# A decoder trunk on one core: parameters loaded late, first weights loaded early, eight unused matmuls

## The chip, the cores and the metric

The kernel runs on one core of one Trainium2 chip. TensorE does matmuls and transposes, VectorE, ScalarE and GpSimd do the element-wise work, and SyncE (SP) issues nearly all loads; each engine works through its own instructions in order. The metric is the device time of one execution in microseconds (us), as the median of several runs.

## The reference

One layer of a hybrid decoder in float32, 1024 tokens of width 1024:

```python
h = rms_norm(x, norm_mix_g[l], NORM_EPS)
z = h @ w_in[l]                          # 1024 x 2048: pool inputs, q, k, v
y_pool = pooling_mixer(zp, pool_w[l], pool_scale[l])
lam = exp(sum(lambda_q1 * lambda_k1)) - exp(sum(lambda_q2 * lambda_k2)) + lam_init
o = diff_attention(q, k, v, lam, rel_bias)   # 4 heads, two softmax maps each
o = rms_norm(o, subln_g[l], SUBLN_EPS) * (1.0 - lam_init)
x = x + concatenate([y_pool, o]) @ w_out[l]
h = rms_norm(x, norm_ffn_g[l], NORM_EPS)
gu = h @ ffn_w_in[l]                     # 1024 x 5632
g = causal_depthwise_conv(gu[..., :D_FF], ffn_conv_w[l], ffn_conv_b[l])
x = x + (silu(g) * gu[..., D_FF:]) @ ffn_w_out[l]
return rms_norm(x, norm_final_g, NORM_EPS)
```

## The kernel before, in words

Each float32 product is made of three matmuls: operands are split into a high part (a cast, on ScalarE) and a low part (a subtraction, on GpSimd for weights, on VectorE for what comes out of a PSUM bank), and `mm3` (L143 to L145) adds high x high, high x low and low x high.

The kernel goes through these stages: the row tiles of x are normalised and transposed, and the q, k and v projections of head 0 run as tiles become ready; then attention of four heads, interleaved with the other projections and the pooling; the output projection in three groups; the second normalisation; the gated MLP, upward and downward. The names and lines that the change touches are all in the first stage.

Row tiles. x0 to x7 are 128 tokens each (tile `x`, four buffers, so x4 needs x0's buffer, and x6 that of x2). For each tile ScalarE squares and sums it (L116, `sq`), VectorE and ScalarE make the reciprocal root (L118 to L122, L108 to L111), VectorE scales the tile (L130; for x5 and x7 L127, with GpSimd multiplying by the norm's weights at L128). TensorE transposes it in two groups of four (L139) into PSUM tiles `tp` (two buffers), ScalarE copies each out as `hTh` (L83) and VectorE makes `hTl` (L84). A buffer of `tp` is free again when its low part is made.

First projections. `q0`, `k0` and `v0` (tiles `raw`, `whi`, `wlo`) are the weights of head 0. `first_units` runs their projections `z_q`, `z_k`, `z_v`: for the first four tiles in pairs of tiles (256 columns), for the last four at once (512 columns). They are copied out at L285, L286 (q), L299 to L301 (k) and L314, L317 (v, with one more transpose `tpv`).

Small parameters. `load_params` loads the relative bias `rel_bias` (`rb`), a one-hot table (`oh`), a row with the lambdas and the far bias broadcast to all partitions (`flat`), and rows with convolution and norm weights (`prow`). `small_params` makes of them a bias row `r_ps` (L194, written to DRAM and read back per head as `hank`), the transposed parameters `prm` (L199, L200), `recfar` (L202) and the factor `nlam` (L206 to L211). The first attention step needs the bias and `nlam`.

Order. `LOADS` is the order in which the first loads are issued. The order of the rest is that in which the code records it, rearranged by a scheduler; `tc.high_priority()` moves a piece forward. `ws` holds `raw` once and `whi`, `wlo` twice, so the weights of head 1 wait for the last use of q0's.

Of the kernel before, what the change touches and what calls it, by code (L numbers as in the profile page):

```python
# [19 lines left out]
NT = S // P  # L20
# [11 lines left out]
QK = 10  # L32
OUT_GROUPS = ((3, 2), (1, 0, 4), (5, 6, 7))
FIRST = ("q0", "k0", "v0")
LOADS = "x0 g x1 x2 q0 k0 s x3 v0"
SHARE = (5, 7)
PLAN = ("b0 a00 a01 q1 a02 k1 v1 a03 b1 p3 a10 q2 a11 a12 v2 a13 k2 p2 b2 a20 a21 q3 p0 a22 p1 a23 v3 k3 "
        "b3 a30 a31 a32 a33")
# [4 lines left out]
def trunk_kernel(ctx, tc, x, norm_mix_g, w_in, pool_w, rows, line, rel_bias, w_out, norm_ffn_g,  # L43
                 ffn_w_in, ffn_w_out, norm_final_g, onehot, out):
    nc = tc.nc
# [16 lines left out]
    def slot(dt, name):  # L62
        return slots.tile([P, S], dt, tag="y", name=name)

    def sc_ps(name):
        return ps_a.tile([P, 512], F32, tag="sc", bufs=3, name=name)

    def pv_ps(name):
        return ps_a.tile([P, 512], F32, tag="pv", bufs=1, name=name)

    def tp_ps(name):
        return ps_a.tile([P, 4, P], F32, tag="tp", bufs=2, name=name)
# [5 lines left out]
    def split(hi, lo, src, lo_eng=None):  # L78
        nc.scalar.copy(hi, src)  # L79
        (lo_eng or nc.gpsimd).tensor_tensor(lo, src, hi.bitcast(F32), op=ALU.subtract)  # L80

    def psplit(hi, lo, src):
        nc.scalar.copy(hi, src)  # L83
        nc.vector.tensor_tensor(lo, src, hi.bitcast(F32), op=ALU.subtract)  # L84
# [9 lines left out]
    def split_w(raw, name):  # L94
        if name == "v0":
            hi, lo = [slot(F32R, f"{n}_{name}").rearrange("p (k c) -> p k c", c=P) for n in ("whi", "wlo")]
        else:
            hi = ws.tile([P, KC, P], F32R, tag="whi", name=f"whi_{name}")
            lo = ws.tile([P, KC, P], F32R, tag="wlo", name=f"wlo_{name}")
        split(hi, lo, raw)  # L100
        return hi, lo
# [23 lines left out]
    def scale_rows(dst, src, r, g, share):  # L125
        if share:
            nc.vector.tensor_scalar(dst, src, r, None, op0=ALU.mult)  # L127
            nc.gpsimd.tensor_tensor(dst, dst, g, op=ALU.mult)  # L128
        else:
            nc.vector.scalar_tensor_tensor(dst, src, r, g, op0=ALU.mult, op1=ALU.mult)  # L130

    def to_channels(xn, hi, lo, t, name):
        for q in range(2):
            if name == "f" and q:
                tp = sc_ps(f"tp_{name}_{t}_{q}").rearrange("p (k c) -> p k c", c=P)
            else:
                tp = tp_ps(f"tp_{name}_{t}_{q}")
            for k in range(4):
                nc.tensor.transpose(tp[:, k, :], xn[:, (4 * q + k) * P:(4 * q + k + 1) * P], ident)  # L139
            psplit(hi[q][:, :, t * P:(t + 1) * P], lo[q][:, :, t * P:(t + 1) * P], tp)  # L140
# [26 lines left out]
    def load_x(t):  # L167
        xt = att.tile([P, D], F32, tag="p", bufs=4, name=f"x_{t}")
        nc.sync.dma_start(xt, x[t * P:(t + 1) * P, :])
        return xt  # L170


    prow = att.tile([96, P], F32, tag="ln", bufs=2, name="prow")
    flat = att.tile([P, 276], F32, tag="hank", bufs=1, name="flat")
# [4 lines left out]
    oh = att.tile([33, 512], F32, tag="ln", bufs=2, name="oh")  # L179

    def load_params():
        nc.vector.memset(rb[32:33, :], NEG)
        nc.sync.dma_start(rb[0:32, :], rel_bias)
        nc.sync.dma_start(oh, onehot)
        nc.sync.dma_start(flat, line.to_broadcast((P, 276)))
        nc.sync.dma_start(prow[0:93, :], rows)
# [5 lines left out]
    def small_params():  # L192
        r_ps = sc_ps("r_ps")
        nc.tensor.matmul(r_ps[0:NH, :], rb, oh, start=True, stop=True)  # L194
        r_sb = att.tile([NH, 512], F32, tag="vt", bufs=1, name="r_sb")
        nc.vector.tensor_copy(r_sb, r_ps[0:NH, :])
        nc.sync.dma_start(scratch, r_sb)
        prm_ps = sc_ps("prm_ps")
        nc.tensor.transpose(prm_ps[:, 0:93], prow[0:93, :], ident[0:93, 0:93])  # L199
        nc.vector.tensor_copy(prm[:, 0:93], prm_ps[:, 0:93])  # L200
        nc.vector.tensor_scalar(gsub, prm[:, 92:93], 1.0 - LAM_INIT, None, op0=ALU.mult)
        nc.vector.tensor_copy(recfar, flat[:, 256:276])  # L202
        lam_s = const.tile([P, 2], F32, name="lam_s")
        lam_p = att.tile([P, 64], F32, tag="tb", bufs=1, name="lam_p")
        for j in range(2):
            nc.vector.tensor_tensor_reduce(lam_p, lam_in[:, 2 * j, :], lam_in[:, 2 * j + 1, :], 1.0, 0.0,  # L206
                                           ALU.mult, ALU.add, lam_s[:, j:j + 1])
        lam_e = const.tile([P, 2], F32, name="lam_e")
        nc.scalar.activation(lam_e, lam_s, AF.Exp)
        nc.vector.tensor_tensor(nlam, lam_e[:, 1:2], lam_e[:, 0:1], op=ALU.subtract)  # L210
        nc.vector.tensor_scalar(nlam, nlam, -LAM_INIT, None, op0=ALU.add)  # L211
# [6 lines left out]
    def load_step(s):  # L218
        if s[0] == "x":
            xs[int(s[1])] = load_x(int(s[1]))  # L220
        elif s == "g":
            nc.sync.dma_start(g_bc, norm_mix_g.to_broadcast((P, D)))
        elif s == "s":
            load_params()
        else:
            first_raw[s] = load_raw(w_in_src(dict(q0=4, k0=8, v0=12)[s]), s)

    xs, first_raw, first_w, first_evac, first_ps = {}, {}, {}, {}, {}
    for s in LOADS.split():
        load_step(s)  # L230
# [45 lines left out]
    def q_sink(h):  # L276
        q = [att.tile([P, S], F32R, tag="qk", bufs=QK, name=f"q{h}_{c}") for c in range(2)]

        def evac(half, ps):
            cs = slice(half * 512, half * 512 + 512)  # L280
            for c in range(2):
                hi = q[c][64 * c:64 * c + 64, cs]
                lo = q[c][64 - 64 * c:128 - 64 * c, cs]
                src = ps[64 * c:64 * c + 64, :]
                nc.scalar.mul(hi, src, SC)  # L285
                nc.vector.scalar_tensor_tensor(lo, src, SC, hi.bitcast(F32), op0=ALU.mult, op1=ALU.subtract)  # L286
        return q, evac

    def k_sink(h):
        kh = [(slot(F32R, f"kh{h}_{c}") if h == 1 else  # L290
               att.tile([P, S], F32R, tag="qk", bufs=QK, name=f"kh{h}_{c}")) for c in range(2)]
        kl = slot(F32R, f"kl{h}") if h == 1 else att.tile([P, S], F32R, tag="qk", bufs=QK, name=f"kl{h}")

        def evac(half, ps):
            cs = slice(half * 512, half * 512 + 512)
            for c in range(2):
                src = ps[64 * c:64 * c + 64, :]
                own = kh[c][64 * c:64 * c + 64, cs]
                nc.scalar.copy(own, src)  # L299
                nc.scalar.copy(kh[c][64 - 64 * c:128 - 64 * c, cs], src)  # L300
                nc.vector.tensor_tensor(kl[64 * c:64 * c + 64, cs], src, own.bitcast(F32), op=ALU.subtract)  # L301
        return (kh, kl), evac

    def v_sink(h):
        vh = att.tile([P, S], F32R, tag="qk", bufs=QK, name=f"vh{h}")
        if h == 1:
            vl = slot(F32R, f"vl{h}")
        else:
            vl = att.tile([P, S], F32R, tag="pl" if h == 3 else "qk", bufs=3 if h == 3 else QK, name=f"vl{h}")
        vh, vl = [a.rearrange("p (t e) -> p t e", e=P) for a in (vh, vl)]  # L310

        def evac(half, ps):
            vt = att.tile([P, 512], F32, tag="vt", bufs=1, name=f"vt{h}_{half}")
            nc.scalar.copy(vt, ps)  # L314
            tp = mm_ps(f"tpv{h}_{half}").rearrange("p (t e) -> p t e", e=P)
            for j in range(4):
                nc.tensor.transpose(tp[:, j, :], vt[:, j * P:(j + 1) * P], ident)  # L317
            psplit(vh[:, 4 * half:4 * half + 4, :], vl[:, 4 * half:4 * half + 4, :], tp)
        return (vh, vl), evac

    for t in range(NT):
        if t == 1:
            first_w.update({n: split_w(first_raw[n], n) for n in FIRST})
            q0, first_evac["q0"] = q_sink(0)
            k0, first_evac["k0"] = k_sink(0)
            v0, first_evac["v0"] = v_sink(0)
            small_params()
        if t not in xs:
            xs[t] = load_x(t)
        xt = xs[t]  # L330
        sq = att.tile([P, S], F32, tag="pl", bufs=3, name=f"sq_{t}")
        r = row_rstd(xt, sq, f"m{t}")
        scale_rows(xt, xt, r, g_bc, t in SHARE)
        with tc.high_priority():
            to_channels(xt, hTh, hTl, t, "m")
        if t % 2 == 1:
            first_units(t // 2)

# [163 lines left out]
    x1 = [None] * NT  # L502
# [317 lines left out]
```

## Time and profile before

| | |
|---|---|
| median of 3 runs | 1118.35 us (1118.02 to 1118.36) |
| the profiled execution: time | 1118.18 us |
| its span, first to last instruction | 1116.4 us |
| TensorE busy | 1068.5 us (96%) |
| VectorE busy | 725.4 us (65%) |
| ScalarE busy | 475.9 us (43%) |
| GpSimd busy | 337.4 us (30%) |
| mean granted TensorE clock | 0.984 |

Times in the rows are counted from the start of the span, so the profiled execution has 1.78 us around it. In the profile PE is TensorE, PEld its weight loads, DVE is VectorE, ACT is ScalarE, POOL is GpSimd, and SPq is SyncE's queue, on which loads are issued. A matmul's time in a row is from its start to the modelled end; since matmuls overlap, their pace is read from one start to the next. A granted clock below 1 is a stretch in which the clock was held at its lower level for a part of the time; the first 25 us show 1.00 in that column although the matmuls' pace there is that of the lower level, so the pace is what is read there.

### The profile page before, as it was taken

What the parts mean: (1) busy time and instruction counts of PE and PEld (TensorE: products, weight loads), DVE (VectorE), ACT (ScalarE), POOL (GpSimd) and SP (SyncE); (2) the same over time, 40 slices, a digit from 0 to 9 for tenths busy, and PEclk for the clock granted to TensorE, in tenths of its full rate; (3) what the DMA queues carried; (4) which work ended last, traced back from release to release, by engine and by line L of the source; (5) the groups of instructions that cost most, each with busy time, mean ns of one, the idle gap of its engine ahead of it and who ended that gap; (6) DMA issues with size and microseconds to landing.
All of it is one profiled execution on the core that took longest, in us unless ns stands there. A gap on an engine that the chain in (4) does not pass through costs nothing.

```text
span 1116.4 us, 13587 instructions
## 1 busy us (share of the span) xinstructions
PE 1068.5 (96%) x5011; PEld 885.4 (79%) x5011; DVE 725.4 (65%) x1213; ACT 475.9 (43%) x775; POOL 337.4 (30%) x240
## 2 busy tenths in 40 slices
PE   5999999999899897899999999999999999999997
PEld 4988888887778585778888888888888788888885
DVE  6556786878796589476657656755765655544545
ACT  5557476655762355244434443433444222111123
POOL 3232242432740237133322222221314322221211
PEclk9999999999899898899999999999999999999999
DMA  7111110100586642123122222222247632212112
GB/s 233 36 44 33 43 46 19 43 20 8 208 281 218 199 170 76 57 86 98 62 95 95 79 73 94 77 86 85 76 132 254 236 113 98 86 63 95 38 49 103
DMA packets 85990, 111.76 MB, mean 100 GB/s; under 512 B 3618, under 2 KB 66303, under 8 KB 85924
## 3 DMA queue, kind: packets, MB, share of 16 engines
q1 hardware_dynamic: 79300, 86.78, 24.2%
q10 hardware_dynamic: 6624, 24.12, 5.6%
q8 instruction: 39, 0.64, 0.2%
q14 instruction: 27, 0.22, 0.1%
HBM read 82.57 MB, written 28.32 MB: 99 GB/s over the span
## 4 chain that ended last, share of the span: by engine, by line
PE 82%; DVE 8%; ACT 3%; issue 3%; DMA 2%; POOL 1%; SPq 1%; DVEq 0%; ACTq 0%; POOLq 0%
PE p L644 36%; PE fo L741 7%; PE fo L742 7%; PE fo L743 7%; PE o L533 2%; PE o L532 2%; PE o L531 2%; PE z_q L144 1%; PE z_q L145 1%; PE z_q L143 1%; PE s L353 1%; PE s L352 1%; PE tpa L402 1%; PE z_p L143 1%; PE z_p L144 1%
## 5 line engine op out<-in xcount | busy, mean ns | idle before, releaser
L741 PE MATMUL fo<-w,a 128*128 128x512 f32 x352 | 137.3, 390 | 2.7 <-DVE xr L744 2.7
L744 DVE TENSOR_TENSOR xr<-xr,fo 128x512 f32<-128x512 f32 x112 | 75.9, 684 | 97.0 <-PE fo L743 96.3
L742 PE MATMUL fo<-w,a 128*128 128x512 f32 x352 | 137.0, 389 | 0.0
L743 PE MATMUL fo<-w,a 128*128 128x512 f32 x352 | 137.0, 389 | 0.0
L80 POOL TENSOR_TENSOR w<-rw,w 128x1024 fp32r<-128x1024 f32 x22 | 61.3, 2794 | 156.3 <-ACT w L79 156.3
L622 POOL TENSOR_TENSOR sa<-rg 128x512 f32<-128x512 f32 x22 | 33.4, 1519 | 209.6 <-DMA rg<-in_ffn_w_in_dram 209.6
L741 PEld LDWEIGHTS fo<-w,a 128*128 128x128 f32 x352 | 66.1, 188 | 17.5 <-DVE xr L744 3.9
L80 POOL TENSOR_TENSOR ul<-ru,uh 128x1024 fp32r<-128x1024 f32 x22 | 57.9, 2632 | 69.9 <-PE p L644 35.9
L743 PEld LDWEIGHTS fo<-w,a 128*128 128x128 f32 x352 | 66.1, 188 | 13.9
L742 PEld LDWEIGHTS fo<-w,a 128*128 128x128 f32 x352 | 66.1, 188 | 13.7
L79 ACT CAST a<-ra 128x1024 fp32r<-128x1024 f32 x22 | 23.2, 1052 | 119.8 <-PE fo L743 62.8
L362 ACT ACTIVATE p<-p,nm 128x128 f32<-128x128 f32 (+7 forms) x64 | 49.6, 776 | 50.4 <-DVE nm L361 47.7
L644 PE MATMUL p<-t4h,gt 128*128 128x512 f32 x176 | 58.0, 391 | 1.7 <-DVE g L669 1.7
L531 PE MATMUL o<-woh,yh 128*128 128x512 f32 x128 | 52.7, 417 | 5.0 <-ACT yh L79 4.2
L623 DVE TENSOR_TENSOR sa<-sa,ru 128x512 f32<-128x512 f32 x22 | 39.9, 1813 | 22.7 <-POOL sa L622 22.7
L349 POOL CAST qz<-q 64x128 fp32r<-64x128 f32 x64 | 23.6, 371 | 97.1 <-PE s L353 90.2
L533 PE MATMUL o<-woh,yl 128*128 128x512 f32 x128 | 51.9, 407 | 0.6 <-DVE yl L80 0.6
L532 PE MATMUL o<-wol,yh 128*128 128x512 f32 x128 | 52.2, 409 | 0.3 <-POOL wol L80 0.3
L79 ACT CAST uh<-ru 128x1024 fp32r<-128x1024 f32 x22 | 23.2, 1054 | 68.2 <-PE p L644 66.9
L80 DVE TENSOR_TENSOR a<-ra,a 128x1024 fp32r<-128x1024 f32 x22 | 42.9, 1948 | 12.2 <-ACT a L79 11.8
L671 DVE TENSOR_TENSOR g<-eb,p 128x512 f32<-128x512 f32 x22 | 15.1, 687 | 54.9 <-PE p L644 54.9
L534 DVE TENSOR_TENSOR x<-x,o 128x512 f32<-128x512 f32 x48 | 32.7, 684 | 20.4 <-PE o L533 18.5
(264 smaller groups left out, 3082.7 us busy)
## 6 DMA issues: line engine op xcount, KB each, us to landing
x_rows<-x ACTq DMA_DIRECT2D x24, 512.0 KB, 3.3
ru<-in_ffn_w_in_dram SPq DMA_DIRECT2D x22, 512.0 KB, 4.1
rg<-in_ffn_w_in_dram SPq DMA_DIRECT2D x22, 512.0 KB, 3.9
act_rows<-cv ACTq DMA_DIRECT2D x22, 512.0 KB, 3.0
rw<-in_ffn_w_out_dram SPq DMA_DIRECT2D x22, 512.0 KB, 4.2
ra<-act_rows SPq DMA_DIRECT2D x22, 512.0 KB, 3.4
x<-in_x_dram SPq DMA_DIRECT2D x16, 512.0 KB, 5.8
x<-x_rows SPq DMA_DIRECT2D x16, 512.0 KB, 3.9
```

The costliest lines, as they stand in the source:

```text
L79: nc.scalar.copy(hi, src)
L80: (lo_eng or nc.gpsimd).tensor_tensor(lo, src, hi.bitcast(F32), op=ALU.subtract)
L362: nc.scalar.activation(s[:, 0:w], s[:, 0:w], AF.Exp, bias=negm[:, c:c + 1], accum_out=sums[:, c:c + 1])
L531: nc.tensor.matmul(ps, yh[:, ts], wh[:, cs], start=n == 0, stop=False)
L532: nc.tensor.matmul(ps, yh[:, ts], wl[:, cs], start=False, stop=False)
L533: nc.tensor.matmul(ps, yl[:, ts], wh[:, cs], start=False, stop=n == len(wo) - 1)
L623: nc.vector.tensor_tensor(s2, s1, a11, op=ALU.subtract)
L644: nc.tensor.matmul(ps, w[:, k, :], h[:, k, :], start=start and k == 0 and n == 0, stop=k == 3 and n == 2, skip_group_check=not start)
L741: nc.tensor.matmul(ps, ah[:, ts], wh[:, cs], start=n == 0, stop=False)
L742: nc.tensor.matmul(ps, ah[:, ts], wl[:, cs], start=False, stop=False)
L743: nc.tensor.matmul(ps, al[:, ts], wh[:, cs], start=False, stop=n == len(ops) - 1)
L744: nc.vector.tensor_tensor(xr[t][:, cs], xr[t][:, cs], ps, op=ALU.add)
```

## The change

The first weights are loaded between the row tiles instead of after them, and the step `s` (`load_params`) leaves the list of first loads. Eight matmuls of q0's weights with themselves, whose result nothing reads, stand behind the splits of the first weights. `load_params` and `small_params` are called after the seventh row tile (x6) has been scaled and transposed; three one-column copies from x6 into `oh`, `prow` and `flat` make the loads of these three wait for it.

```diff
@@ -32,7 +32,7 @@
-LOADS = "x0 g x1 x2 q0 k0 s x3 v0"
+LOADS = "x0 g x1 q0 x2 k0 x3 v0"
@@ -321,10 +321,12 @@
     for t in range(NT):
         if t == 1:
             first_w.update({n: split_w(first_raw[n], n) for n in FIRST})
+            idle, wq = pv_ps("idle"), first_w[FIRST[0]][0]
+            for n in range(8):
+                nc.tensor.matmul(idle, wq[:, 0, :], wq[:, 0:4, :], start=True, stop=True)
             q0, first_evac["q0"] = q_sink(0)
             k0, first_evac["k0"] = k_sink(0)
             v0, first_evac["v0"] = v_sink(0)
-            small_params()
@@ -333,6 +335,12 @@
         with tc.high_priority():
             to_channels(xt, hTh, hTl, t, "m")
+        if t == NT - 2:
+            nc.vector.tensor_copy(oh[:, 0:1], xt[0:33, 0:1])
+            nc.vector.tensor_copy(prow[:, 0:1], xt[0:96, 0:1])
+            nc.vector.tensor_copy(flat[:, 0:1], xt[:, 0:1])
+            load_params()
+            small_params()
         if t % 2 == 1:
             first_units(t // 2)
```

On SP, from the fourth issue of the program on, before (x_117 is x2, x_128 x3, x_451 x4, x_482 x5; raw_q_857 is head 1's):

```order
L169 DMA x_117<-in_x_dram 128x1024
L91 DMA raw_q_119<-in_w_in_dram 128x8x128
L91 DMA raw_k_121<-in_w_in_dram 128x8x128
L183 DMA rb<-in_rel_bias_dram 32x4
L184 DMA oh<-in_onehot_dram 33x512
L185 DMA flat<-in_line_dram 128x276
L186 DMA prow<-in_rows_dram 93x128
L169 DMA x_128<-in_x_dram 128x1024
L91 DMA raw_v_130<-in_w_in_dram 128x8x128
L169 DMA x_451<-in_x_dram 128x1024
L91 DMA raw_q_857<-in_w_in_dram 128x8x128
```

And in the changed kernel (x_119 is x2, x_123 x3, then x_437, x_468, x_500 and x_557 for x4 to x7):

```order
L91 DMA raw_q_117<-in_w_in_dram 128x8x128
L169 DMA x_119<-in_x_dram 128x1024
L91 DMA raw_k_121<-in_w_in_dram 128x8x128
L169 DMA x_123<-in_x_dram 128x1024
L91 DMA raw_v_125<-in_w_in_dram 128x8x128
L183 DMA rb<-in_rel_bias_dram 32x4
L169 DMA x_437<-in_x_dram 128x1024
L91 DMA raw_q_869<-in_w_in_dram 128x8x128
L169 DMA x_468<-in_x_dram 128x1024
L169 DMA x_500<-in_x_dram 128x1024
L169 DMA x_557<-in_x_dram 128x1024
L184 DMA oh<-in_onehot_dram 33x512
```

The loads of `flat` and `prow` follow behind `oh`. The three have moved from ahead of x3 to behind x7; `rb`, which no copy holds, stands behind the v weights.

On VectorE, where `flat` is first read, before (x_115 is x1, x_117 x2; rt and rr are steps of the reciprocal root):

```order
L84 TENSOR_TENSOR hTl_111<-tp_m_1_154,hTh_109 128x4x128
L108 TENSOR_SCALAR rt_m_311<-var_m_305,rs_m_307 128x1
L202 COPY recfar<-flat 128x20
L206 ISA lam_p,lam_s<-flat 128x64
L206 ISA lam_s 128x1
L109 TENSOR_SCALAR rt_m_311<-rt_m_311 128x1
L196 COPY r_sb<-r_ps 4x512
L206 ISA lam_p,lam_s<-flat 128x64
L206 ISA lam_s 128x1
L111 TENSOR_SCALAR rr_m_314<-rs_m_307,rt_m_311 128x1
L200 COPY prm<-prm_ps 128x93
L130 SCALAR_TENSOR_TENSOR x_117<-x_117,rr_m_314,g_mix 128x1024
```

And in the changed kernel, where x_557 is x7 (the row above the first here is the last of the three copies from x6):

```order
L84 TENSOR_TENSOR hTl_110<-tp_m_0_454,hTh_108 128x4x128
L118 TENSOR_SCALAR var_m_562<-ss_m_560 128x1
L202 COPY recfar<-flat 128x20
L206 ISA lam_p,lam_s<-flat 128x64
L206 ISA lam_s 128x1
L108 TENSOR_SCALAR rt_m_568<-var_m_562,rs_m_564 128x1
L206 ISA lam_p,lam_s<-flat 128x64
L206 ISA lam_s 128x1
L109 TENSOR_SCALAR rt_m_568<-rt_m_568 128x1
L111 TENSOR_SCALAR rr_m_571<-rs_m_564,rt_m_568 128x1
L127 TENSOR_SCALAR x_557<-x_557,rr_m_571 128x1024
L84 TENSOR_TENSOR hTl_111<-tp_m_1_461,hTh_109 128x4x128
```

The steps on `flat` have moved from ahead of x2's scaling to ahead of x7's, and x4's second low part (the last row) stands behind them.

On TensorE, at the end of the first-half projections in the changed kernel (x_500 is x6, x_557 x7; in before r_ps and prm_ps are the third and fourth rows of the program, and the first bias matmul `hp` and a score pair stand where the first L144 of z_q_1 is here):

```order
L194 MATMUL r_ps<-oh,rb 4x512
L199 MATMUL prm_ps<-ident,prow 128x93
L139 MATMUL tp_m_1_524<-ident,x_500 128x128 x4
L139 MATMUL tp_m_0_575<-ident,x_557 128x128 x4
L317 MATMUL tpv_0_430<-ident,vt_0_428 128x128 x4
L143 MATMUL z_q_1_589<-hTh_108,whi_q_156 128x512
L143 MATMUL z_v_1_649<-hTh_108,whi_v_164 128x512
L139 MATMUL tp_m_1_582<-ident,x_557 128x128 x4
L144 MATMUL z_q_1_589<-hTl_110,whi_q_156 128x512
```

The parameter matmuls have moved from the start of the program to this place, and `hp` with the first scores to behind the second-half projections.

## Rows read from the trace of the kernel before

**Rows 1.** Timeline, TensorE, 15 to 26: start, duration, engine, line, what; then idle before.
```profile
15.05 1.92 PE L139 MATMUL tp_m<-ident,x 128*128 128x128 f32 x8
...
18.64 0.58 PE L143 MATMUL z_q<-hTh,whi_q 128*128 128x256 f32 x1 [1.68 <-ACT hTh L83]
...
24.32 0.41 PE L143 MATMUL z_q<-hTh,whi_q 128*128 128x256 f32 x1
...
24.54 0.41 PE L145 MATMUL z_k<-hTh,wlo_k 128*128 128x256 f32 x1
...
25.75 0.28 PE L143 MATMUL z_q<-hTh,whi_q 128*128 128x256 f32 x1
...
25.87 0.28 PE L144 MATMUL z_q<-hTl,whi_q 128*128 128x256 f32 x1
```
**Rows 2.** Windows: stretch, us, PE, PEld, DVE, ACT, POOL busy (count), clock, DMA.
```profile
20.00:25.00 5.00, 4.96 (x24) 4.79 (x24) 4.31 (x14) 3.60 (x12) 2.00 (x1) 1.00 0.32 106
...
30.00:35.00 5.00, 5.00 (x45) 5.00 (x44) 3.35 (x9) 3.52 (x10) 0.42 (x2) 1.00 0.31 105
```
**Rows 3.** Timeline, VectorE and GpSimd, 12 to 18.
```profile
12.15 3.26 POOL L80 TENSOR_TENSOR wlo_q<-raw_q,whi_q 128x1024 fp32r<-128x1024 f32 x1 [10.50 <-ACT whi_q L79]
...
14.27 1.17 DVE L202 COPY recfar<-flat 128x20 f32<-128x20 f32 x1 [0.29 <-DMA flat<-in_line_dram]
...
15.36 0.21 DVE L206 CUSTOM_DVE_ANT_0 lam_p<-flat 128x64 f32<-128x64 f32 x1
15.38 2.41 POOL L80 TENSOR_TENSOR wlo_k<-raw_k,whi_k 128x1024 fp32r<-128x1024 f32 x1
...
16.17 1.70 DVE L206 CUSTOM_DVE_ANT_0 lam_p<-flat 128x64 f32<-128x64 f32 x1
```
**Rows 4.** The chain of waits, 0 to 120: start, us, what.
```profile
9.53 4.72 DMA flat<-in_line_dram
...
26.98 0.44 PE tp_m L139 x4
```
**Rows 5.** DMA issues, 0 to 60: tile, queue, count, KB each, us to landing.
```profile
hank<-bias_row SPq DMA_DIRECT2D x2, 192.0 KB, 3.0
```
**Rows 6.** Timeline, the loads of x and ScalarE's squares.
```profile
15.63 1.06 ACT L116 ACTIVATE sq<-x 128x1024 f32<-128x1024 f32 x1 [1.73 <-DMA x<-in_x_dram]
...
25.71 4.66 SPq L169 DMA_DIRECT2D x<-in_x_dram  x2
...
29.25 1.06 ACT L116 ACTIVATE sq<-x 128x1024 f32<-128x1024 f32 x1 [1.20 <-DMA x<-in_x_dram]
```
**Rows 7.** Timeline, ScalarE and VectorE, 36 to 42.
```profile
36.41 0.59 ACT L285 ACTIVATE q<-z_q 64x512 fp32r<-64x512 f32 x1 [1.11 <-PE z_q L145]
...
37.12 0.69 DVE L286 SCALAR_TENSOR_TENSOR q<-z_q,q 64x512 fp32r<-64x512 f32 x1
...
41.34 0.68 DVE L301 TENSOR_TENSOR kl<-z_k,kh 64x512 fp32r<-64x512 f32 x1 [1.32 <-ACT kh L300]
```
**Rows 8.** Timeline, all engines, 46 to 66.
```profile
46.81 0.44 PE L144 MATMUL z_q<-hTl,whi_q 128*128 128x512 f32 x1
...
53.94 0.39 PE L145 MATMUL z_q<-hTh,wlo_q 128*128 128x512 f32 x1
...
55.37 2.40 POOL L80 TENSOR_TENSOR wlo_q<-raw_q,whi_q 128x1024 fp32r<-128x1024 f32 x1 [8.04 <-ACT whi_q L79]
...
61.65 1.05 ACT L79 CAST whi_k<-raw_k 128x1024 fp32r<-128x1024 f32 x1 [1.58 <-DMA raw_k<-in_w_in_dram]
...
64.57 0.66 PE L317 MATMUL tpv<-ident,vt 128*128 128x128 f32 x4 [1.17 <-ACT vt L314]
...
65.31 0.40 PE L143 MATMUL z_q<-hTh,whi_q 128*128 128x512 f32 x1
```
**Rows 9.** Waits of TensorE, 64 to 280: us in total, times, longest.
```profile
PE tpv L317 <- ACT vt L314: 1.2, 1, 1.2
```
**Rows 10.** Windows, 290 to 295 (columns as in rows 2).
```profile
290.00:295.00 5.00, 3.98 (x12) 3.17 (x13) 4.28 (x8) 3.30 (x8) 5.00 (x4) 0.50 0.67 210
```

## The prediction

> **What bounds the kernel now.** I read the page's busy shares first: TensorE is at work for 1068.5 of 1116.4 us, so whatever delays its instructions near the start is paid at the end, unless a later wait absorbs it. Then the timeline of the first 66 us, the chain of waits, and five-microsecond windows. Four things are to be seen there.
>
> First, TensorE does its first projection matmul at 18.64, and until about 25 it runs at 1.2 GHz: 256-column matmuls start 0.22 apart at 24.32 and 24.54, and 0.12 apart at 25.75 and 25.87 [rows 1]. The windows say the same, 24 matmuls in 20 to 25 and 45 in 30 to 35 [rows 2]. Ahead of the rise stood about 4 us of unbroken projections; the eight transposes at 15.05 had not lifted it [rows 1].
>
> Second, what held the start back is VectorE. The small parameters stand there in front of the third row tile: the copy of 20 columns (L202) takes 1.17 and one of the two 64-column products (L206) 1.70, both while GpSimd splits weights, 12.15 to 15.41 and 15.38 to 17.79 [rows 3], and `flat`, for which the copy waited, had landed 4.72 after its issue [rows 4].
>
> Third, the end of the row-tile stage is a ladder of ScalarE and VectorE steps: q is copied out of its bank at 36.41, its low part made at 37.12, and so on through q's other half, both halves of k and the last transposes, k's first low part at 41.34 [rows 7]; the second-half projections run without a break only from 46.81 [rows 8].
>
> Fourth, there is a chain that needs no row tile: when q0's weights are used for the last time (53.94 + 0.23 = 54.17), whi_q of head 1 can be made, wlo_q follows on GpSimd at 55.37, only then the next weights are loaded, ScalarE waits 1.58 for them at 61.65, and behind that copy stand the evacuations for which TensorE waits 1.17, at 64.57 [rows 8]. From the last use of q0's weights to that matmul it is 64.57 - 54.17 = 10.4 us, whatever TensorE does meanwhile.
>
> **The change, part by part.** The sum is made against the profiled execution's own 1118.18 us (span 1116.4 and 1.78 around it); the median of the runs, 1118.35, is 0.17 above.
>
> *Weights between the row tiles, parameters out of the way.* x3 and the v weights lose four small loads in front of them; x3's square starts at 15.63 after a wait for its DMA [rows 6], and I take about 14.5 instead, since the 0.25 MB of small loads go and its issue moves up. ScalarE then finishes the square at 15.65 (1.06 and 0.1 for its accumulator) and copies x1's transposes, so the first projection matmul is at about 16.3 instead of 18.64. VectorE, without L202 and L206, has x2 (in by about 11, squared behind x1's first copy) scaled at 16.5 and frees x1's first transpose bank at 17.3. Unbroken work starts there, 3 us before now (20.2). This is the gross gain.
>
> *The eight matmuls.* They wait for whi_q (about 10.5 to 10.8) and are 512 columns wide: at 1.2 GHz, by 0.22 for 256 columns, 8 x 0.43 = 3.4 us, to about 14.1. x1 is scaled at about 13.6, so its transposes are held 0.5 us; that is covered, as ScalarE is busy with x3's square till 15.65 anyway. What the matmuls give is the clock: if it is at 2.4 GHz at 17.3, the first 20 projections take 20 x 0.12 = 2.4 instead of 4.4. Whether it is, no row of before shows: the bounds are 0 and 2.0 us for this step. I take the clock as raised, since 3.4 us of matmuls, the transposes and the first projections stand ahead of it, nearer to the 4 us that stood ahead of the rise now than to the broken work of 13 to 20.
>
> *Where the gain is lost.* x6 is issued when x2's second transposes are done (one buffer set of four): now 25.71, and squared at 29.25 [rows 6], 3.5 later. In the changed order these transposes stand behind 20 projections: 17.3 + 0.44 (four transposes, [rows 4]) + 2.4 + 0.44 = 20.6. So x6 is squared at 24.1 and scaled by 28.6: 1.4 for square and variance, 1.2 for the root's six small steps, 1.3 for the scaling, and 0.6 behind a low part of x3. Then come the three one-column copies, about 0.1 each, behind the low part of x3 (28.6 to 29.25), and only they release the parameter loads: `oh` about 29.5, `flat` 29.9. `flat` lands 4.72 after its issue in the crowd of the start [rows 4], `hank`, of like size, after 3.0 on a quiet queue [rows 5]; x7 is already in by about 30.2, so I take 2.9: 32.8. VectorE is in order, and L202 stands there in front of x7's statistics, its scaling, the low parts of x4 and x5 and q's low part. It has nothing to do from 31.5 to 32.8: a new wait of about 1.3.
>
> The price of L202 and L206 there lies between 0.5 for all (the other product of the pair took 0.21) and 1.17 + 0.21 + 1.70 = 3.1 [rows 3]. GpSimd has finished x5's product by 28.5 (scaled at 26.1, and 2.4 for 1024 columns) and has x7's only after VectorE's scaling, so I take 0.5. The Trainium skill says why the two rows are so far apart: in "SBUF — State Buffer", section "Who interferes with whom", VectorE and GpSimd share one port pair that one of them holds for its whole instruction while the other waits. The rows agree: 16.17 + 1.70 ends with the GpSimd row that began at 15.38. By that rule the cost is 0.5 while GpSimd is idle and up to 3.1 if a split is running.
>
> From there: x7 scaled 34.4 to 35.1, x4's and x5's low parts to 36.4, q's first low part at 36.5 (now 37.12). The ladder [rows 7] then runs at its own pace, as it does now: 37.12 to 46.81 is 9.7 us, of which 0.8 went to the bias matmul and a score pair that the new order puts later, and some 0.7 are saved by a shorter wait for k. 36.5 + 9.7 - 0.8 - 0.7 = 44.7 for the matmul now at 46.81. TensorE has come to the end of the first-half projections at about 38.4, does r_ps and prm_ps there (about 1 us, hidden in the wait), and idles for about 4 us in all between 39 and 44.7. Of the 5 us that earlier work and clock could give, some 3 are stopped here.
>
> Then the fourth chain: q0's weights are last used 35 matmuls in, at 0.23 each (32 now, 46.81 to 54.17), so 44.7 + 8.0 = 52.7; plus 10.4 is 63.1 for the matmul now at 64.57. TensorE waits about 1.4 there, since it has only the bias matmul and a score pair (0.9) left over. z_q of head 1 starts at 63.8 instead of 65.31 [rows 8], with one pair and more of scores (0.45) still owed: 65.31 - 63.8 - 0.45 = 1.1 us gained. From 66 to 280 TensorE waits for less than 2 us in all (four lines of waits, 3.0 in all, of which the largest, 1.2, is the one just counted [rows 9]), so 1.1 arrives at the output projection and, all later waits being counted from there, at the end. 1118.18 - 1.1 = 1117.1; with 0.17 that is 1117.2.
>
> **The rivals.**
> *VectorE doesn't hold TensorE.* If `flat` lands by 31.5, 1.3 more is gained (2.4 in all); if the ladder, too, closes up behind TensorE, the second half starts at about 41 and the fourth chain alone is left: 41 + 8.0 + 10.4 = 59.4, and 64.57 - 59.4 - 0.45 = 4.7. For it: the ladder's steps are 0.6 to 0.7 each and now partly wait for k's projections. Against: VectorE's order puts everything for x7 behind `flat`. Times 1113.5 to 1116, middle 1114.8.
>
> *VectorE held by the parameters (slower).* The same place at the prices of the start: `flat` 4.72 instead of 2.9 and L202 and L206 3.1 instead of 0.5, 4.4 us more, so -3.3: 1121.5. It ends on the other side of no change once it costs 1.1 more than I take, and beyond 0.2% from 3.3 more. For it: the start shows just these prices [rows 3, 4]. Against: DMA and GpSimd are quiet at 30 to 34.
>
> *The clock rises no sooner than with the first projections.* x6 and all behind it 2 us later: 1.1 - 2.0 = -0.9, 1119.2. For it: the transposes at 15.05 did not lift it [rows 1], and after the eight matmuls come transposes again and two gaps.
>
> *The output projection.* The order there is changed too, and the clock falls in four stretches between 285 and 457, as in 290 to 295, granted at half [rows 10]. In 290 to 298 some 6.5 us of work ran at half speed: one fall more or less is worth about 3.3. That gives 1114 or 1120.5. Nothing in before says which.
>
> **How the numbers follow.** About 0.2% (2.2 us) is what a measurement of this kernel can tell from no change. Forecast 0.42; VectorE not holding 0.22; VectorE held 0.11; clock late 0.12; output projection 0.13, half each way. Faster by over 0.2% (below 1116.1): 0.20 of the second, 0.07 of the last and 0.10 from the low edge of the forecast's own spread, 0.37. Slower (above 1120.6): 0.11 and 0.05 and 0.02 of the clock's, 0.18. The rest, 0.45, within. The range runs from nearly the full 4.7 gained, 1113.5, to 1121.2, near the held case.
>
> **What would show it.** In the changed profile: projections 0.12 apart from 17.5 on; x6 issued near 20.6; VectorE idle before L202, released by `flat`; the second half unbroken from about 44.7; the wait for tpv still there, near 63. If 256-column matmuls are 0.22 apart past 20, the clock step is wrong; if VectorE doesn't wait before L202, or the second half starts before 43, the loss is wrong; if z_q of head 1 starts near 63.8 and the end is not about 1 us earlier, it is the output projection.

## The result: 0.6% slower, and outside the forecast

The changed kernel takes 1125.72 us (median of 4 runs, 1123.53 to 1126.39), the kernel before 1118.34; the ratio is 1.0064 with a 95% interval of 1.005 to 1.0078. The forecast was 1117.2 in a range of 1113.5 to 1121.2, with a chance of 0.18 for slower. In a later set of runs the changed kernel had 1125.37, the kernel before 1118.07.

The profiled execution has 1125.85 us and a span of 1124.1. Busy times hardly moved; what grew is time in which TensorE waits or runs at the lower clock. First the page of the changed kernel, section on busy times:

```profile
PE 1071.9 (95%) x5019; PEld 886.7 (79%) x5019; DVE 726.0 (65%) x1216; ACT 476.1 (42%) x775; POOL 336.1 (30%) x240
```

Next its windows, with the columns of [rows 2]:

```profile
15.00:20.00 5.00, 3.57 (x23) 2.96 (x22) 4.59 (x12) 4.89 (x12) 3.50 (x2) 1.00 0.95 301
20.00:25.00 5.00, 5.00 (x45) 5.00 (x44) 4.71 (x12) 2.12 (x6) 0.51 (x1) 1.00 0.34 105
...
40.00:45.00 5.00, 3.44 (x17) 2.29 (x18) 3.58 (x9) 4.06 (x8) 0.54 (x2) 0.88 0.00 0
45.00:50.00 5.00, 4.88 (x23) 3.92 (x22) 4.03 (x7) 2.76 (x5) 0.00 (x0) 0.78 0.02 6
65.00:70.00 5.00, 2.95 (x14) 2.42 (x13) 2.60 (x9) 3.72 (x9) 2.87 (x3) 0.77 0.39 88
70.00:75.00 5.00, 5.00 (x24) 4.22 (x23) 1.37 (x6) 0.41 (x2) 0.55 (x2) 0.89 0.20 60
```

45 matmuls in 20 to 25 against 24 before [rows 2]: the early start and the raised clock are there. But TensorE is at work for only 3.44 of the 5 us from 40, and twice, from 44 and from 68, the clock is granted at half for some 3 us, right behind such idle time. The sum had some 4 us of idle time between 39 and 44.7, but no fall of the clock.

The timeline of the changed kernel, several engines, in order of time:

```profile
10.91 2.39 POOL L80 TENSOR_TENSOR wlo_q<-raw_q,whi_q 128x1024 fp32r<-128x1024 f32 x1 [9.25 <-ACT whi_q L79]
12.28 2.10 DVE L130 SCALAR_TENSOR_TENSOR x<-x,rr_m,g_mix 128x1024 f32<-128x1024 f32 x1
...
18.40 0.66 PE L139 MATMUL tp_m<-ident,x 128*128 128x128 f32 x4 [1.42 <-DVE hTl L84]
...
19.13 0.28 PE L143 MATMUL z_q<-hTh,whi_q 128*128 128x256 f32 x1
19.25 0.28 PE L144 MATMUL z_q<-hTl,whi_q 128*128 128x256 f32 x1
...
27.46 2.39 POOL L128 TENSOR_TENSOR x<-x,g_mix 128x1024 f32<-128x1024 f32 x1 [6.96 <-issue]
28.59 2.35 DVE L130 SCALAR_TENSOR_TENSOR x<-x,rr_m,g_mix 128x1024 f32<-128x1024 f32 x1
...
32.06 0.34 SPq L185 DMA_DIRECT2D flat<-in_line_dram  x1
...
35.20 0.18 DVE L202 COPY recfar<-flat 128x20 f32<-128x20 f32 x1 [2.38 <-DMA flat<-in_line_dram]
35.28 0.22 DVE L206 CUSTOM_DVE_ANT_0 lam_p<-flat 128x64 f32<-128x64 f32 x1
...
36.19 0.75 DVE L127 TENSOR_SCALAR x<-x,rr_m 128x1024 f32<-128x1024 f32 x1
37.02 2.37 POOL L128 TENSOR_TENSOR x<-x,g_mix 128x1024 f32<-128x1024 f32 x1 [3.57 <-DVE x L127]
37.46 1.95 DVE L210 TENSOR_TENSOR nlam<-lam_e 128x1 f32<-128x1 f32 x1
40.06 0.66 PE L139 MATMUL tp_m<-ident,x 128*128 128x128 f32 x4 [1.45 <-DVE nlam L211]
40.10 0.69 DVE L286 SCALAR_TENSOR_TENSOR q<-z_q,q 64x512 fp32r<-64x512 f32 x1
...
43.99 1.97 PE L139 MATMUL tp_m<-ident,x 128*128 128x128 f32 x8 [1.49 <-DVE hTl L84]
...
48.18 0.50 PE L144 MATMUL z_q<-hTl,whi_q 128*128 128x512 f32 x1
...
67.27 0.74 PE L317 MATMUL tpv<-ident,vt 128*128 128x128 f32 x4 [2.05 <-ACT vt L314]
```

At 19.13 the projections already start 0.12 apart, before only from 25.75 [rows 1]. q's first low part (L286) starts at 40.10, before at 37.12 [rows 7]; the unbroken second half at 48.18, before 46.81; tpv at 67.27, before 64.57 [rows 8]. What pushes L286 in the end is a VectorE step on one element per partition: L210 (nlam) takes 1.95, and ends at 39.41, when GpSimd's x7 product ends (37.02 + 2.37 = 39.39).

The waits of TensorE from 10 to 80 in the changed kernel (us in total, times, longest):

```profile
PE tp_m L139 <- DVE hTl L84: 2.9, 2, 1.5
PE tpv L317 <- ACT vt L314: 2.1, 1, 2.1
PE tp_m L139 <- DVE nlam L211: 1.4, 1, 1.4
```

The wait for tpv has grown from 1.2 [rows 9], and those for hTl and nlam are new.

All kernels at five places of TensorE's program and three of VectorE's ladder, each from its profiled execution (start times in us, and for nlam the time that the step takes; "second half" is the first L144 of z_q with 512 columns, "last z_k" that of head 3, "p" the matmuls of the upward MLP stage, L644 in the kernel before). The median is that of all executions; the profiled one took 1115.69 for early_params, 1115.46 for late_only, 1121.67 for hold_clock, 1124.32 for five_unused and 1130.42 for q_first, and is within 0.5 of the median for the others:

| kernel | median | L202 | q's low part | nlam (L210) takes | second half | head 1's z_q | last z_k | first p | last p |
|---|---|---|---|---|---|---|---|---|---|
| before | 1118.34 | 14.27 | 37.12 | 0.14 | 46.81 | 65.31 | 278.49 | 428.23 | 869.39 |
| changed | 1125.72 | 35.20 | 40.10 | 1.95 | 48.18 | 68.13 | 284.96 | 435.24 | 877.03 |
| no_unused | 1112.75 | 35.59 | 36.20 | 0.15 | 45.18 | 64.33 | 279.72 | 428.11 | 864.16 |
| early_params | 1117.26 | 14.82 | 36.43 | 0.14 | 46.57 | 65.30 | 278.38 | 426.28 | 867.19 |
| late_only | 1113.58 | 34.58 | 34.99 | 1.89 | 45.80 | 65.24 | 280.59 | 428.74 | 866.72 |
| loads_free | 1111.72 | 18.25 | 34.58 | 0.15 | 44.77 | 63.83 | 279.30 | 426.58 | 863.25 |
| nlam_pool | 1122.83 | 37.41 | 40.38 | (GpSimd) | 48.24 | 67.67 | 283.15 | 433.25 | 874.27 |
| hold_clock | 1123.69 | 35.26 | 40.16 | 1.95 | 48.02 | 67.20 | 282.58 | 431.78 | 873.40 |
| five_unused | 1125.76 | 37.36 | 42.24 | 1.93 | 50.32 | 69.62 | 285.11 | 433.87 | 875.74 |
| two_unused | 1122.14 | 36.86 | 38.62 | 1.00 | 46.89 | 66.01 | 281.39 | 431.85 | 873.45 |
| q_first | 1128.37 | 38.32 | 40.75 | 0.15 | 50.17 | 68.49 | 288.87 | 440.07 | 881.89 |
| loads_free_plain | 1119.28 | 15.38 | 36.53 | 0.14 | 45.91 | 65.08 | 280.35 | 428.76 | 870.38 |
| unused_same_order | 1114.27 | 37.12 | 37.73 | 0.15 | 46.71 | 66.10 | 281.47 | 429.80 | 865.83 |
| changed_again | 1125.37 | 37.34 | 42.22 | 1.93 | 50.48 | 70.46 | 285.82 | 436.27 | 876.59 |

Against the kernel before, the changed one is 2.82 late at head 1's z_q, 6.47 at the last z_k, 7.01 at the first p and 7.64 at the last: the loss is made ahead of 285.

### The profile page after: what moved, and what is told of

It reads as the page before. It is cut to its first block, busy times and chain, and to the rows that moved or that the text cites. A ratio compares the mean times of both kernels' runs of the same rounds, so it can differ in the third digit from the quotient of the medians.

```text
span 1124.1 us, 13611 instructions
## 1 busy us (share of the span) xinstructions
PE 1071.9 (95%) x5019; PEld 886.7 (79%) x5019; DVE 726.0 (65%) x1216; ACT 476.1 (42%) x775; POOL 336.1 (30%) x240
## 4 chain that ended last, share of the span: by engine, by line
PE 77%; DVE 11%; DMA 4%; ACT 3%; issue 3%; POOL 2%; SPq 0%; DVEq 0%; ACTq 0%; POOLq 0%
PE p L652 35%; PE fo L749 7%; PE fo L750 7%; PE fo L751 7%; PE o L541 2%; PE o L540 1%; PE o L539 1%; PE s L360 1%; PE z_p L143 1%; PE z_p L144 1%; PE s L361 1%; PE z_p L145 1%; PE tpa L410 1%; PE z_k L145 1%; PE z_k L143 1%
## 5 line engine op out<-in xcount | busy, mean ns | idle before, releaser
L80 DVE TENSOR_TENSOR a<-ra,a 128x1024 fp32r<-128x1024 f32 x22 | 42.5, 1933 | 11.5 <-ACT a L79 10.9
```

## The experiments

The kernel before ran again beside them, with medians of 1117.22, 1118.01, 1117.73 and 1118.07; ratios are against those.

**First set: the parts alone.** *no_unused* leaves out the eight matmuls:

```diff
-            idle, wq = pv_ps("idle"), first_w[FIRST[0]][0]
-            for n in range(8):
-                nc.tensor.matmul(idle, wq[:, 0, :], wq[:, 0:4, :], start=True, stop=True)
```

> The changed kernel without the eight unused matmuls. Theory (the parameter steps on VectorE beside x7 push the last steps of the row tiles, TensorE idles and its clock falls twice): projections 0.22 apart until about 24 again, x6 loaded up to 2 us later, both late falls of the clock still there, time 1125.5 to 1128. Rival A (the unused matmuls and the weights loaded early do the harm, through VectorE and GpSimd at x1 and x2): at most 1122. Rival B (the loss is in the order of the output projection and behind): the stretch up to 200 us as in the changed kernel, the time anywhere.

1112.75, ratio 0.9962 (0.995 to 0.9974): 13 less than with them. The theory (1125.5 to 1128) missed; the time fits rival A (at most 1122), but the place doesn't, nor is it the matmuls' own length. x6 is squared 1.28 later without them (26.59 against 25.31; 16 matmuls run in 20 to 22.5 instead of 24), but its scaling runs alone and takes 1.28, where the changed kernel needs 2.35 beside GpSimd: in both it ends at 30.94. So the 1.3 that the changed kernel was ahead by are lost there. In both x7 is squared at 31.5, and L202 stands at 35.20 (changed) or 35.59; only from there on VectorE's instructions stand in another order. The scheduler counts the eight matmuls as TensorE time, and so, as I read it, takes q's bank for ready later; in the changed kernel it puts x7's scaling, two low parts and nlam ahead of q's low part, in this one q and nlam first. The timeline of no_unused, VectorE and GpSimd, and the start of the second half:

```profile
25.98 2.41 POOL L128 TENSOR_TENSOR x<-x,g_mix 128x1024 f32<-128x1024 f32 x1 [6.11 <-PE tp_m L139]
...
29.66 1.28 DVE L130 SCALAR_TENSOR_TENSOR x<-x,rr_m,g_mix 128x1024 f32<-128x1024 f32 x1
...
35.59 0.18 DVE L202 COPY recfar<-flat 128x20 f32<-128x20 f32 x1 [1.13 <-DMA flat<-in_line_dram]
...
36.20 0.68 DVE L286 SCALAR_TENSOR_TENSOR q<-z_q,q 64x512 fp32r<-64x512 f32 x1
...
37.65 0.15 DVE L210 TENSOR_TENSOR nlam<-lam_e 128x1 f32<-128x1 f32 x1
37.71 0.80 DVE L127 TENSOR_SCALAR x<-x,rr_m 128x1024 f32<-128x1024 f32 x1
...
38.74 2.40 POOL L128 TENSOR_TENSOR x<-x,g_mix 128x1024 f32<-128x1024 f32 x1
...
45.18 0.50 PE L144 MATMUL z_q<-hTl,whi_q 128*128 128x512 f32 x1 [0.53 <-DVE hTl L84]
```

From L202 to the second half it is 9.59 here and 12.98 in the changed kernel.

*early_params* puts the parameters back (`LOADS = "x0 g x1 q0 x2 k0 s x3 v0"`, `small_params()` at the second row tile, no copies).

> The changed kernel with load_params and small_params back at their old places (the weights between the row tiles and the unused matmuls stay). Theory: flat and nlam are done before x2, the second-half projections run without a break before 46 and the clock does not fall there; time 1115.5 to 1118. Rival A (weights and unused matmuls do the harm): 1122 or more. Rival B (output projection): 1122 or more with a first stage that ends early.

1117.26, ratio 1.0003 (0.9991 to 1.0016), as the theory had the time, though the second half starts at 46.57 and not before 46. Weights between tiles and unused matmuls together are worth nothing clear of noise: 278.38 at the last z_k, 278.49 before. The clock fell to 0.50 between 20 and 22.5, after TensorE had been at work for 1.84 of the 5 us from 15.

*late_only* is the kernel before with the late parameters alone (`LOADS = "x0 g x1 x2 q0 k0 x3 v0"`, the block at `t == NT - 2`).

> The kernel before with the parameters alone moved behind the seventh row tile (weights in their old order, no unused matmuls). Theory: VectorE waits for flat and nlam there as in the changed kernel, the second half begins at 48 or later, time 1122 to 1128. Rival A: 1117 to 1119, no loss. Rival B: the time anywhere, the first stage no later than before.

1113.58, ratio 0.9966 (0.9955 to 0.9977): the theory's 1122 to 1128 missed, and its second half at 48 or later, too (45.80, although VectorE waits 1.75 for flat). The first stage is no later than before, as rival B had it. The stages up to the last z_k did lose, though: the last z_k is 2.1 later than before. The gain comes behind it, from first to last p, 438.0 instead of 441.2.

*loads_free* keeps the weights and the eight matmuls; the parameters are loaded behind v0 without copies:

```diff
-LOADS = "x0 g x1 q0 x2 k0 x3 v0"
+LOADS = "x0 g x1 q0 x2 k0 x3 v0 s"
-            nc.vector.tensor_copy(oh[:, 0:1], xt[0:33, 0:1])
...
-            load_params()
             small_params()
```

> The changed kernel without the three copies: the parameters are loaded right behind the v weights, and the steps on them stay behind the seventh row tile in the recorded order. Theory: no wait for flat at 33 to 35, the second half begins 2 us earlier or more than in the changed kernel (48.2) and no fall of the clock, or only one; time 1115 to 1119. Rival A: no change from the changed kernel's 1125.7, within 1. Rival B: the first stage ends earlier, the time stays above 1123.

1111.72, ratio 0.9954 (0.9942 to 0.9967), below the expected range; this version beats both kernels. The scheduler moves the steps on flat up to 18.25, the second half starts at 44.77 and no clock falls there. Still its last z_k is 0.8 later than before's; first to last p is 436.7.

**Second set: collision, clock, order.** *nlam_pool* does L210 and L211 on GpSimd:

```diff
-        nc.vector.tensor_tensor(nlam, lam_e[:, 1:2], lam_e[:, 0:1], op=ALU.subtract)
-        nc.vector.tensor_scalar(nlam, nlam, -LAM_INIT, None, op0=ALU.add)
+        nc.gpsimd.tensor_tensor(nlam, lam_e[:, 1:2], lam_e[:, 0:1], op=ALU.subtract)
+        nc.gpsimd.tensor_scalar(nlam, nlam, -LAM_INIT, None, op0=ALU.add)
```

> The changed kernel with the two small steps on nlam (L210, L211) on GpSimd, ahead of x7's product there, instead of on VectorE; TensorE's order and that of the other VectorE steps stay. Theory (VectorE's order there, with nlam taking 1.95 beside GpSimd's x7 product, holds q's first low part, TensorE idles and its clock falls): q's first low part at about 38.2 instead of 40.1, the wait of 1.45 ahead of x6's transposes gone, the second half unbroken by 46.5 instead of 48.2, time 1121 to 1123.5. Rival (the collision is not what holds it): 1125 or more.

1122.83, ratio 1.0047 (1.0035 to 1.0059): the expected gain of 3, but the times inside missed, since here the clock was at 0.50 from 19.4 to 22.9 and flat landed 2.2 later (L202 at 37.41). Counted from L202, q's low part comes after 2.97 instead of 4.90 and the second half after 10.83 instead of 12.98. So 1.9 to 2.2 us are nlam beside GpSimd's product.

*hold_clock* puts six unused matmuls into the idle time before 44:

```diff
+        if t == NT - 1:
+            for n in range(6):
+                nc.tensor.matmul(idle, wq[:, 0, :], hTl[1][:, :, 4 * P:5 * P], start=True, stop=True)
```

> The changed kernel with six more unused matmuls (512 columns each) in the second of TensorE's two idle stretches before the second half, between prm_ps and x6's second transposes; the order of the first stage is else the same, that of the output projection is another. Theory: the granted clock stays at 1.00 between 43 and 48, the second half runs unbroken from about 46.7 instead of 48.2, head 1's z_q starts at 66 to 66.8 instead of 68.1; time 1120 to 1124. Rival (the fall of the clock costs nothing, since VectorE's steps end no earlier): second half still at 48, z_q of head 1 at 67.8 or later.

1123.69, ratio 1.005 (1.0033 to 1.0068), runs from 1120.38 to 1127.06. Its windows:

```profile
40.00:45.00 5.00, 4.77 (x25) 2.95 (x26) 3.58 (x9) 4.00 (x8) 0.53 (x2) 1.00 0.00 0
45.00:50.00 5.00, 4.17 (x23) 2.97 (x22) 3.91 (x7) 2.63 (x5) 0.00 (x0) 1.00 0.04 11
65.00:70.00 5.00, 3.49 (x20) 2.98 (x19) 2.90 (x11) 3.29 (x9) 2.61 (x3) 1.00 0.45 131
```

The clock stayed up, and the second half still began at 48.02: the rival was right on the first fall up to there, VectorE and ScalarE set that start. From there to head 1's z_q it is 19.18 instead of 19.95, so the fall did cost 0.8 behind it; z_q is 0.93 earlier, at 67.20, between what theory and rival had. The second fall is gone, too: 2.4 at the last z_k for both falls. In three of its six executions the mean granted clock was 0.978 to 0.981, in the profiled one 0.986, so the median doesn't measure a clock that is held throughout.

*five_unused* has `range(5)`; *two_unused* has `range(2)`.

> The changed kernel with five unused matmuls instead of eight; the instructions then stand in the same order on every engine. Theory (the order does it): second half at 47.5 to 48.5, both falls of the clock, time 1124 to 1127. Rival A (the unused matmuls themselves, by their length or by the clock they raise): somewhere between 1112.75 without them and 1125.7 with eight, 1117 to 1121.

1125.76, ratio 1.0073 (1.0061 to 1.0084), the time that the order theory gave; on every engine the instructions other than the unused matmuls run in the order of the changed kernel. Two details missed: the second half starts at 50.32, and the clock falls once, from 42.5 to 49.3, instead of twice. Here the projections run at the low pace up to 22 (15 matmuls in 20 to 22.5, 24 in the changed kernel), L202 stands 2.2 later, and the end is the same.

> The changed kernel with two unused matmuls; TensorE's order in the first stages is that of the kernel without any, the order at the output projection and the second norm is another one. Theory (two separate losses, the first stage and the order of the output projection): the last k projection of head 3 at 279 to 281 as without them (279.7), and from there to the end 3 to 6 us more than without them, time 1116 to 1119. Rival (the first stage alone counts): 1112 to 1114.

1122.14, ratio 1.0041 (1.0028 to 1.0053), 3 above the range. TensorE's order is that of no_unused from 41 us on, but for the second norm (388 to 465); ahead of 41 the projections stand in another order. The last z_k is 1.7 later (L202 stands 1.3 later, nlam took 1.00, and VectorE's order is again another), first p to last p 441.6 instead of 436.05. The waits of TensorE from 424 to 870, us in total, times, longest; first two_unused:

```profile
PE p L652 <- ACT t3h L83: 3.0, 1, 3.0
PE tp_b L586 <- DVE x L579: 2.7, 1, 2.7
PE p L652 <- DVE b11l L84: 2.3, 1, 2.3
PE p L652 <- DVE g L677: 1.8, 1, 1.8
```

and no_unused, where t3h and b11l are not waited for:

```profile
PE tp_b L583 <- DVE x L576: 2.7, 1, 2.7
PE tp_t L583 <- DVE t4l L84: 2.3, 1, 2.3
PE p L649 <- DVE g L674: 1.7, 1, 1.7
```

These two waits are 3.0 + 2.3 = 5.3, but no_unused waits 2.3 for t4l inside the same stage. From the first p to the last, the windows (columns as in [rows 2]; first two_unused, then no_unused) show

```profile
431.85:873.45 441.60, 432.65 (x1890) 356.14 (x1890) 284.42 (x290) 176.91 (x214) 129.67 (x70) 0.98 0.30 98
428.11:864.16 436.05, 430.97 (x1898) 355.08 (x1897) 285.12 (x290) 178.59 (x216) 132.10 (x73) 0.99 0.31 99
```

441.60 - 432.65 = 8.95 of idle time on TensorE against 436.05 - 430.97 = 5.08: 3.9 of the 5.6 are waits. In the rest the clock has a part, at 0.50 for 14.7 us of the stage instead of 6.7; how much is not shown. All ten profiles whose stage takes 440.3 to 441.9 wait for t3h and b11l, the one before and the changed one among them; the four with 436.0 to 438.0 don't.

**Third set.** *q_first* makes x7's scaling wait for q:

```diff
+        if t == NT - 1:
+            nc.vector.scalar_tensor_tensor(r, q0[0][:, 0:1].bitcast(F32), 0.0, r, op0=ALU.mult, op1=ALU.add)
```

> The changed kernel, eight unused matmuls and late parameters included, with one small VectorE step (0.15) that makes x7's scaling wait for q's first low part; the planner then puts nlam and q's low part ahead of x7 on VectorE. Theory (the order of VectorE's steps there is the first loss): from flat's landing to the start of q's first low part 2 to 2.5 us instead of 4.9, nlam's step 0.2 instead of 1.95, second half unbroken by 45 to 46.5 (48.2 in the changed kernel), head 1's z_q by 64 to 66 (68.1), last k projection of head 3 at 280 to 282.5 (285.0); time 1118 to 1122.5, less by 5 if the planner's order at the second norm is the shorter one. Rival A (the unused matmuls do it themselves): second half at 47.5 or later, last k projection at 284 or later.

1128.37, ratio 1.009 (1.0074 to 1.0106): missed. Two local numbers came as expected, 2.43 from L202 to q's low part and 0.15 for nlam. But the clock was at 0.50 from 17.6 to 24.4 in the profiled run, so that L202 stood at 38.32; x7 was scaled at 41.67; and the second half began 11.85 after L202, 1.1 sooner than in the changed kernel and not 3. Putting q first by force moves the wait to x7. Behind it this kernel is the slowest of all: from head 1's z_q to the last z_k it takes 220.4, where ten others take 215.3 to 215.5; TensorE is idle for 4.85 of them (2.48 in no_unused), and the clock falls once more (0.67 in 265 to 270). Why is open.

*loads_free_plain* is loads_free with s ahead of v0 and no unused matmuls.

> The kernel with the parameters loaded ahead of the v weights, no copies and no unused matmuls; the planner gives it the first stage of the kernel with free loads, and at the second norm the order of the changed kernel and of the one before. Theory (second loss: that order makes the upward MLP stage 5 us longer): last k projection of head 3 at 278.5 to 280.5, first to last p matmul 440.5 to 442 instead of 436.7, waits for t3h and b11l of 3.0 and 2.3 there; time 1115.5 to 1118.5. Rival (the first stage alone sets the time): 1110.5 to 1113.

1119.28, ratio 1.0017 (1.0008 to 1.0025). The last z_k at 280.35, p from first to last 441.6, with the waits for t3h (3.0) and b11l (2.3): all as the theory had it, the time 0.8 above its range. Its first stage is near that of loads_free, not the same: L202 stands at 15.38, the second half at 45.91, and TensorE's order differs up to 42 us. But the last z_k is only 1.05 later, and the p stage 4.9 longer. So 441 or 436 goes with the order at the second norm, not with the first stage.

**Fourth set: two controls.** *unused_same_order* has 28 unused matmuls ahead of x0's transposes, and every other instruction in no_unused's order:

```diff
+            idle = pv_ps("idle")
+            for n in range(28):
+                nc.tensor.matmul(idle[:, 0:128], ones, ones, start=True, stop=True)
```

> The changed kernel with 28 unused matmuls of 128 columns (about as many columns as in the eight) that need no weights and stand ahead of x0's transposes; every engine's other instructions then stand as in the kernel without any. Theory (not the unused matmuls themselves but the order they bring about makes the time): within 1.5 of that kernel's 1112.75. Rival A (unused matmuls cost time or clock wherever they stand): 1116 or more.

1114.27, ratio 0.9966 (0.9955 to 0.9978): 1.52 above no_unused, at the very edge of what the theory allowed; as ratios the two are 0.9966 and 0.9962. From L202 to the second half 9.59 again. These matmuls ran from 1.54, where nothing else wants TensorE, so it is no test of eight at 10.9.

> The changed kernel once more, beside the others on this chip. Theory: 1123.5 to 1127 as before; the granted clock between 17 and 23 may be at either level, since two other kernels with the same start had it at 0.50 there, and where it is, flat lands 1.5 to 3 later than 35.2 and the later falls of the clock are others. Rival: the same trace as at first, to 0.3, up to 70.

1125.37, ratio 1.0068 (1.0055 to 1.0081), and another trace: its windows

```profile
15.00:20.00 5.00, 2.86 (x16) 2.35 (x15) 4.33 (x11) 4.56 (x10) 3.67 (x2) 0.77 0.94 301
20.00:25.00 5.00, 5.00 (x40) 5.00 (x40) 4.75 (x12) 2.35 (x8) 0.28 (x1) 0.89 0.18 35
...
45.00:50.00 5.00, 3.89 (x16) 3.37 (x17) 4.39 (x9) 4.23 (x8) 0.00 (x0) 0.50 0.02 3
65.00:70.00 5.00, 3.31 (x17) 2.50 (x16) 1.49 (x3) 3.10 (x5) 1.99 (x1) 1.00 0.32 92
```

show a clock that fell back at 17.7 already, a fall at 45, and none at 68. Head 1's z_q is 2.3 later than in the first profile, the last z_k 0.9, the time the same.

## Why the prediction was wrong

**The failed step is "Where the gain is lost".** It let q's low part start at 36.5 and the second half at 44.7; they came at 40.10 and 48.18. Two terms were mis-sized.
- The way to L202: 32.8 forecast, 35.20 measured. x6 is issued at 21.91 and scaled by 30.94, where the sum had 20.6 and 28.6: the scalings of x1, x2 and x6 (L130) take 2.10, 1.99 and 2.35 where GpSimd works beside them, not 1.3, the time of one alone, which I took for x6; unbroken work starts at 18.40, not 17.3. flat took 3.1, near the 2.9 taken. L202 and the products cost 0.6, 0.5 forecast.
- From L202 to q's low part: 3.7 forecast, 4.90 measured. nlam had no price in the sum; it takes 1.95 beside the x7 product, and 2.97 is what is left without it (nlam_pool).

The Trainium skill's rule that I drew on for L202, in "SBUF — State Buffer", section "Who interferes with whom", also says that a VectorE step on two tensors with both inputs in SBUF contends with GpSimd's reads. The trace agrees: L210's 1.95 ends with the GpSimd row, while L286, which reads a PSUM bank and SBUF, takes 0.69 beside a GpSimd row in nlam_pool (40.38, product 39.24 to 41.62).

**The order.** Four kernels with the changed kernel's ladder order (changed, changed_again, five_unused, hold_clock) need 12.76 to 13.14 from L202 to the second half, two with no_unused's 9.59. nlam accounts for 2.15 of these 3.4 (nlam_pool). The rest, 1.2, is put down to the order of the other steps by subtraction alone; q_first, which has q first and needs 11.85, shows that it isn't q's place alone. I had this order when I forecast, and costed it as if every step of the ladder kept its old time.

**The eight matmuls.** That the clock is raised at 17.3 was right in the first profile; in the second it fell back from 17.7 to 21.1, with the same total. late_only has 45 matmuls in 20 to 25 without any unused one. What I left out is what the added matmuls do to the scheduler's own clock: in this kernel five and eight bring the order above, two a third one. No run has the eight at 10.9 in no_unused's order, so that the order alone makes the 13 us is argued from the kernels that share an order, not tested.

**The fourth chain** was right: 44.7 to 63.8 is 19.1; no_unused, where the clock holds, has 19.15, the changed kernel 19.95.

**Behind it** I counted 0.45 for a score pair. Between head 1's z_q and the last z_k the kernel before and early_params need 213.1 to 213.2, the ten kernels with moved parameters and no fall of the clock there 215.3 to 215.5, the changed one 216.8 (1.45 more, put down to its fall at 68), q_first 220.4. So 2.2 instead of 0.45; the timelines show 0.5 of waits besides, and some 1.2 stay unlocated. Of 8.8 us of error (7.67 lost, 1.1 gain forecast), 4.3 are made up to head 1's z_q, 3.2 from there to the last z_k, 1.2 behind it.

**The rivals.** "VectorE held by the parameters", given 0.11, has the right place and side; its price was not L202 and L206 but nlam and the scalings. "VectorE doesn't hold TensorE" is out: L202 waits 2.38 for flat. "The clock rises no sooner" came near in the second profile, where the clock fell back and L202 is 2.1 later; the total is the same. "The output projection" was right that a changed order behind the attention matters, though the place is the second norm: it is worth 5 between versions. (Its 3.3 for a fall of the clock rests on 6.5 us of work in 290 to 298; that window has 6.97.) The kernel before and the changed one, however, have p stages of 441.2 and 441.8, so it does not part these two. It does explain why no_unused, late_only, loads_free and unused_same_order beat the kernel before (436.0 to 438.0) although all reach the last z_k later than it does.

## What to carry to other kernels

Where a scheduler orders the program by its own clock, an added instruction costs what its new order costs: lay markers through both traces, and compare kernels with one order from a marker on before a part gets the credit. A control that has the added work at its own place in the old order would tell the two apart; unused_same_order has the order, but not the place. Let a VectorE step with two SBUF inputs end no sooner than the GpSimd row that is running when it starts, however few elements it has: here nlam ended with that row in six profiles.

## What the runs showed of the hardware

- The same program had TensorE's clock at either level after its eight unused matmuls: 1.00 from 15 to 25 in one profile, 0.77 and 0.89 in those five-us windows in the next. In the first, a raised clock was lost again after idle stretches of 1.5 us (at 44) and 2 us (at 68), each time to 0.50 for about 3 us. An idle stretch of that length did not always bring a fall: 1.45 ahead of 40.06 in the same profile, and 1.78 ahead of tpv (64.57) in late_only, left it at 1.00.
- A fall of the clock cost next to nothing up to the place where VectorE and ScalarE set the pace (48.18 with it, 48.02 without), and 0.8 in the unbroken work behind it.
- A subtraction on one element per partition, both inputs in SBUF, took 0.15 alone and 1.95, 1.93, 1.89 or 1.00 beside GpSimd's product, as much as was left of that instruction.
